# Where the operands of a matmul lie in SBUF, and one plain pair fewer in the second feed-forward stage

## The chip, the cores and the metric

The kernel runs on one core of a Trainium2 chip. The metric is the device time of one execution in microseconds (us), as the median of several runs. A profiled execution gives one trace. The engines are called as in the profile: PE is TensorE's matmul, PEld its weight load, DVE is VectorE, ACT is ScalarE, POOL is GpSimd, SP is the queue that issues most of the DMAs.

## The reference

One encoder layer in float32: 512 positions, width 1024. Two gated feed-forward stages of inner width 2752 stand around a mixer (a Fourier mixer and grouped attention with 8 query and 2 key heads).

```python
x = x + 0.5 * swiglu(rms_norm(x, ffn1_norm), ffn1_w_gate, ffn1_w_up, ffn1_w_down)
h = rms_norm(x, mix_norm)
u = h @ w_in
...                                   # Fourier mixer f_out, attention a_out
x = x + jnp.concatenate([f_out, a_out], axis=-1) @ w_out
x = x + 0.5 * swiglu(rms_norm(x, ffn2_norm), ffn2_w_gate, ffn2_w_up, ffn2_w_down)
return rms_norm(x, final_norm)
# swiglu(h, g, u, d) = (silu(h @ g) * (h @ u)) @ d
```

## The kernel before

All activations lie transposed: x is eight tiles of 128 channels by 512 positions. To keep float32 accuracy at the speed of the float32r format, every operand is split in a high part (rounded) and a low part (the rest), and every product is three matmuls: high by high, high by low, low by high (`product`, L144; the same three by hand at L370). ACT rounds the high parts, and DVE subtracts for the low parts (`lows`, L107). A low part can also be made by a DMA that adds onto the negated high part (`rest_by_dma`, L126), which is issued on POOL's queue.

**Places.** `ring` (L83) holds twelve slots of 1024 float32r words per partition. In a feed-forward stage the first eight hold h (`hh`, `hl`: the high and the low part of a norm's input times its gain) at the start, and the others hold converted weights; later all of them hold weights. `gx` (L92) holds x. Each feed-forward stage opens a pool with `at` (L248: the gated activations, seven places of a high and a low part of 512 columns) and `rt` (L249: seven combinations of h's quarters, high and low, 256 columns each). The mixer opens a pool with `more` (two further weight slots), the tables `chan`, `pos`, and its operands `ks`, `vst`, `e`, `qa`, `qb`; a second pool has `ph` and `pl`, the attention's probabilities. Pools lie one behind another in the order in which they are opened, tiles in the order of their allocation.

**A feed-forward stage** (`ffn`, L240) goes through 21 chunks j of 128 inner columns, a gate and an up chunk each (a pair), and a tail of 64 columns ("t"). They come in the four groups of `GROUPS` (L27).
- The first group's pairs are plain (`gate`, L259): 8 x 3 products of 512 columns for the gate chunk and as many for the up chunk. Some of the weights of this part lie in four places of at that are lent (L467). `n_plain`, the number of members of the first group, counts the plain pairs: chunks 0 to n_plain - 1. Beside them the combinations in rt are made (`operands`, L284), four calls spread over the gates.
- The other pairs go by `seven` (L359): gate and up chunk over the two halves of the positions are made from seven products of 4 x 3 matmuls of 256 columns, with rt moving and combinations of the weights (`prepare`, L318) loaded. A group's `seven` runs one chunk ahead of the group.
- After each group come the down products (`down`, L435) of the group's chunks: eight blocks d, each 3 matmuls of 512 columns for a chunk (2 for the tail), with at moving. Their weights are converted by `weights` (L131) when block d begins. In the last group of the second stage the last three blocks run in two halves of 256 columns (`closing`, L1256).

The order on PE and on SP's queue is the order in which the code is written (`in_order`, L100); ACT, DVE and POOL are ordered by a planner with a model of the times. In the mixer all engines follow the written list `ORDER`.

Of the kernel before, what the change touches and what calls it, by code (L numbers as in the profile page):

```python
# [6 lines left out]
F32 = mybir.dt.float32  # L7
# [6 lines left out]
P = 128  # L14
S = 512
D = 1024
KD = D // P
# [6 lines left out]
WARM = 9  # L24
NS = 12

GROUPS = ((0, "t", 1, 2), range(3, 9), range(9, 15), range(15, 21))  # L27
PLACES = 7
HALF = S // 2
USES = "a11", "a12", "s1", "s2", "s4", "s3", "a22"  # L30
# [48 lines left out]
def encoder(ctx, tc, A, out):  # L79
    nc = tc.nc  # L80
    cp = ctx.enter_context(tc.tile_pool(name="const", bufs=1))
    wp = ctx.enter_context(tc.tile_pool(name="weights", bufs=3))
    ring = cp.tile([P, NS, KD * P], F32R, name="ring")  # L83
    taken = []
    tp = ctx.enter_context(tc.tile_pool(name="temps", bufs=2))
    pp = ctx.enter_context(tc.tile_pool(name="psum", bufs=8, space=bass.MemoryType.PSUM))

# [149 lines left out]
            nc.scalar.copy(self.rb[:, t], pss[1][:, t])  # L237
            return pss[0]

    def ffn(norm, after, wgu, wd, wdt, opening, closing):  # L240

        n_ = norm.n
        n_plain = len(GROUPS[0])
        with tc.tile_pool(name=f"act{n_}", bufs=1) as ap, tc.tile_pool(name=f"sums{n_}", bufs=2) as sp:
            at = ap.tile([P, PLACES, 2, S], F32R, name=f"at{n_}")  # L248
            rt = ap.tile([P, 7, 2, KH, HALF], F32R, name=f"rt{n_}")  # L249
            wt = []  # L250
            free, where = list(range(PLACES)), {}
# [7 lines left out]
            def gate(c, between={}, by_dma=False):  # L259
                whi, wlo = weights(wgu[c], f"gu{n_}_{c}", by_dma=by_dma)  # L260
                ps = bank(f"gu{n_}_{c}")
                for k in range(KD):
                    between.get(k, int)()
                    product(ps, whi[:, k, :], wlo[:, k, :], hh[k], hl[k], k == 0, k == KD - 1)
                return ps
# [18 lines left out]
            def operands(rp, i0, i1):  # L284
                for i in range(i0, i1):
                    b = sp.tile([P, 4, HALF], F32, tag="raw_g", name=f"b{n_}_{i}")
                    for o, k in ((0, i), (2, i + KH)):
                        nc.vector.scalar_tensor_tensor(
                            out=b[:, o : o + 2].rearrange("p a b -> p (a b)"), in0=x[k],
                            scalar=gains[:, norm.n, k : k + 1], in1=rp, op0=ALU.mult, op1=ALU.mult,  # L290
                        )
                    b12, b11, b22, b21 = (b[:, o] for o in range(4))
                    t = sp.tile([P, 4, HALF], F32, tag=("s12", "s34")[i % 2], bufs=1, name=f"t{n_}_{i}")
                    for o, (p, q) in enumerate(((b12, b11), (b22, t[:, 0]), (b22, b12), (b21, t[:, 1]))):
                        nc.vector.tensor_tensor(out=t[:, o], in0=p, in1=q, op=ALU.subtract)
                    for src, c in ((b[:, 1:], slice(0, 3)), (t, slice(3, 7))):
                        h, l = rt[:, c, 0, i], rt[:, c, 1, i]
                        nc.scalar.copy(h, src)
                        if src is t or i < 2 or n_:
                            lows(l, src, h)  # L300
                        else:
                            rest_by_dma(l, h, src)
# [132 lines left out]
            def down(d, group, gi):  # L435

                js = [j for j in group if j != "t"]
                whi, wlo = weights(wd[d][:, js[0] : js[-1] + 1, :], f"dn{n_}_{d}_{gi}", len(js))
                w = wt[d // 4][:, d % 4 * P : (d % 4 + 1) * P]

                def steps(ps, t):
                    for i, j in enumerate(group):
                        h, l = (at[:, where[j], o, t] for o in range(2))
                        first, last = i == 0, i == len(group) - 1
                        if j == "t":
                            nc.tensor.matmul(ps[:, t], w, h, start=first, stop=False)
                            nc.tensor.matmul(ps[:, t], w, l, start=False, stop=last)
                        else:
                            k = j - js[0]
                            product(ps[:, t], whi[:, k, :], wlo[:, k, :], h, l, first, last)  # L450
                        yield

                return steps
# [4 lines left out]
                )  # L458

            every = slice(0, S)  # L460
            for gi, group in enumerate(GROUPS):
                last = gi == len(GROUPS) - 1
                ahead = []
                if gi:
                    rest = seven(range(group[0] + 1, min(group[-1] + 2, NF)), ready)
                else:
                    lent = [at[:, i].rearrange("p a b -> p (a b)") for i in range(PLACES - 4, PLACES)]  # L467
                    plain.extend(lent)
                    row = []
                    pss = dict(enumerate(opening(gate, lambda: norm.column([norm.acc]), lambda: row.append(norm.row()))))  # L470
                    back(lent[:2])
                    due, parts, left = [*pss, "t"], list(range(KH)), range(2 * len(pss), 2 * n_plain)
                    pss["t"] = [gate(2 * NF)]
                    tail_weights()
                    for i, c in enumerate(left):
                        pss.setdefault(c // 2, []).append(gate(c, by_dma=not n_ and i > 0))
                        if due:
                            j = due.pop(0)
                            evacuate(at[:, place(j)], n_, pss[j], norm)
                        if c % 2 and c != left[-1]:  # L480
                            due.append(c // 2)
                        while len(parts) * len(left) > (len(left) - 1 - i) * KH:
                            o = parts.pop(0)
                            operands(row[0], o, o + 1)

                    def rest():
                        evacuate(at[:, place(n_plain - 1)], n_, pss[n_plain - 1], norm)

                def added(d, ps):
                    residual(d, ps, every)  # L490
                    if last:
                        (after.sums if closing else after.add)(d)
                    if ahead:
                        f, *a = ahead.pop(0)
                        f(*a)

                waiting = []
                for d in range(KD):
                    if last and closing and d == KD - 3:
                        closing([(e, down(e, group, gi)) for e in range(d, KD)], residual)  # L500
                        break
                    if last and d == KD - 2:
                        back(lent)
                    ps = bank(f"dn{n_}_{d}_{gi}")
                    steps = down(d, group, gi)(ps, every)
                    for _ in range(len(group) - (last and d < 2)):
                        next(steps)
                    waiting.append((d, ps, steps))
                    if d == 1 and not last:
                        ready = prepare(GROUPS[gi + 1][0] + 1)  # L510
                        ahead.extend(ready[1])
                    if d == 0:
                        rest()
                        if last:

                            lent = slots[KD - 2 : KD]
                            plain[2:2] = lent
                            continue
                    for d_, ps, steps in waiting:
                        for _ in steps:  # L520
                            pass
                        added(d_, ps)
                    waiting = []
                for f, *a in ahead:
                    f(*a)
                if not gi:
                    back(lent)
                free.extend(where[j] for j in group)
# [36 lines left out]
    n0, n1 = Norm(0), Norm(1)  # L565
# [84 lines left out]
        return [pss[0:2], pss[2:4]]  # L650

    with in_order():
        ffn(n0, n1, A["wgu1"], A["wd1"], A["wdt1"], opening1, None)


    n2 = Norm(2)
    with tc.tile_pool(name="mix", bufs=1) as mp, tc.tile_pool(name="mixt", bufs=1) as mt:

        more = mp.tile([P, 2, KD * P], F32R, name="more")
        more = [more[:, i, :] for i in range(2)]  # L660
        plain.extend(more)
# [7 lines left out]
        pos = mp.tile([P, 2, 2, 514], F32R, name="pos")  # L669
        odd = mp.tile([1, 258], F32R, name="odd")  # L670
        sc = mp.tile([P, 4, 10], F32, name="sc")


        ops = {}
# [552 lines left out]
    n3 = Norm(3)  # L1227
# [74 lines left out]
        finish(2, 4, n3.rows, ((0,), (1,), (4, 5), (2, 3), (6, 7)))  # L1302

    with in_order():
        ffn(n2, n3, A["wgu2"], A["wd2"], A["wdt2"], lambda gate, column, row: [[gate(0, {KD - 1: column}), gate(1, {3: row})]], closing)


def _order():
# [106 lines left out]
```

## Time and profile before

| | |
|---|---|
| median of 3 runs | 868.52 us (868.05 to 868.54) |
| the profiled execution, its own time | 868.42 us |
| its span (first to last instruction) | 866.4 us |
| mean granted TensorE clock | 0.997 |
| busy, share of the span | PE 99%, PEld 89%, DVE 74%, ACT 53%, POOL 3% |

Groups of instructions are shown as line, engine, operation, output <- inputs, shapes and count, then the busy time in us and the mean duration of one in ns, then the idle time before them and what ended it. Matmuls are pipelined: the duration of one reaches past the start of the next, so the pace of a stretch is its length divided by the number of products in it. A timeline row gives the start and the length in us. A row by stretch gives the length and then for each engine its busy time and count, the granted clock, the DMA engines' mean busy share and the GB/s they moved.

### The profile page before, as it was taken

Reading aid. Unit: us, or ns where it says so; the run is one execution under the profiler, and the core shown is the slowest. Engines: PE = TensorE matmul, PEld = TensorE weight load, DVE = VectorE, ACT = ScalarE, POOL = GpSimd, SP = SyncE. Lnnn points to the kernel's source line nnn. Section 1 sums busy time; section 2 is a strip of 40 time slices with the busy share of each in tenths; the row PEclk is TensorE's granted clock in tenths of the full one; section 3 lists DMA queues with packets and bytes.
Section 4 is the critical chain, followed back from the end, with each engine's and each line's share of the span. In section 5 each row is a group of like instructions: output and inputs, shape, how many; then the busy total and the mean of one; then the engine's idle time right before and its main releaser. Section 6 shows DMA issues by size and latency. Waiting matters only on the chain.

```text
span 866.4 us, 13588 instructions
## 1 busy us (share of the span) xinstructions
PE 858.6 (99%) x5389; PEld 768.2 (89%) x5389; DVE 641.2 (74%) x1003; ACT 462.9 (53%) x771; POOL 29.8 (3%) x32
## 2 busy tenths in 40 slices
PE   9999999999999999999999999999999999999996
PEld 6878998899989998889988888889998999889986
DVE  6998985488746837699998478978974688459544
ACT  7763763267424635677776346535652366326543
POOL 0110000000000000222000000000000000000001
PEclk9999999999999999999999999999999999999998
DMA  7664322323233113414010223232323232323212
GB/s 244 164 155 155 116 95 65 116 99 132 73 135 114 44 52 110 146 49 135 32 66 25 98 87 108 85 134 98 110 79 128 92 118 84 98 106 101 74 38 98
DMA packets 30480, 87.94 MB, mean 102 GB/s; under 512 B 3664, under 2 KB 8528, under 8 KB 30288
## 3 DMA queue, kind: packets, MB, share of 16 engines
q1 hardware_dynamic: 28320, 82.87, 28.5%
q0 software_dynamic: 1552, 3.68, 2.1%
q8 instruction: 42, 0.69, 0.3%
q10 hardware_dynamic: 544, 0.52, 0.2%
q14 instruction: 22, 0.18, 0.1%
HBM read 83.39 MB, written 2.10 MB: 99 GB/s over the span
## 4 chain that ended last, share of the span: by engine, by line
PE 97%; DVE 1%; DMA 1%; issue 0%; ACT 0%; POOL 0%; POOLq 0%; SPq 0%; DVEq 0%; ACTq 0%
PE r L370 23%; PE q L370 11%; PE dn L147 8%; PE dn L145 8%; PE dn L146 8%; PE p L370 6%; PE mix L145 3%; PE mix L147 3%; PE mix L146 3%; PE gu L145 3%; PE gu L147 3%; PE gu L146 3%; PE gu L618 3%; PE mix L1106 2%; PE mix L1063 2%; PE mix L913 1%
## 5 line engine op out<-in xcount | busy, mean ns | idle before, releaser
L370 PE MATMUL r<-rt,ring 128*128 128x256 f32 x1632 | 213.2, 283 | 0.0
L370 PEld LDWEIGHTS r<-rt,ring 128*128 128x128 f32 x1632 | 201.8, 188 | 2.4
L147 PE MATMUL dn<-at,ring 128*128 128x512 f32 x303 | 119.7, 395 | 0.2 <-DVE ring L108 0.2
L145 PE MATMUL dn<-at,ring 128*128 128x512 f32 x303 | 119.7, 395 | 0.0
L146 PE MATMUL dn<-at,ring 128*128 128x512 f32 x303 | 119.6, 395 | 0.0
L370 PE MATMUL q<-rt,ring 128*128 128x256 f32 x816 | 107.9, 281 | 0.0
L456 DVE SCALAR_TENSOR_TENSOR gx<-dn,gx 128x512 f32<-128x512 f32 x61 | 42.1, 689 | 82.1 <-PE dn L147 82.0
L370 PEld LDWEIGHTS q<-rt,ring 128*128 128x128 f32 x816 | 101.6, 188 | 0.0
L108 DVE TENSOR_TENSOR ring<-s,ring 128x1024 fp32r<-128x1024 f32 x68 | 82.9, 1221 | 17.6 <-PE r L370 10.6
L137 ACT CAST ring<-raw_dn 128x768 fp32r<-128x768 f32 (+1 forms) x59 | 45.5, 775 | 93.3 <-PE dn L146 77.4
L331 ACT CAST ring<-s 128x1024 fp32r<-128x1024 f32 x68 | 71.4, 1051 | 38.2 <-PE r L370 18.3
L147 PEld LDWEIGHTS dn<-at,ring 128*128 128x128 f32 x303 | 57.0, 188 | 14.3 <-DVE ring L108 0.9
L146 PEld LDWEIGHTS dn<-at,ring 128*128 128x128 f32 x303 | 57.0, 188 | 13.0
L145 PEld LDWEIGHTS dn<-at,ring 128*128 128x128 f32 x303 | 57.0, 188 | 13.0
L108 DVE TENSOR_TENSOR ring<-raw_dn,ring 128x768 fp32r<-128x768 f32 (+1 forms) x59 | 51.8, 880 | 7.2 <-ACT ring L137 6.2
L370 PE MATMUL p<-rt,ring 128*128 128x256 f32 x408 | 53.9, 281 | 0.0
L108 DVE TENSOR_TENSOR ring<-raw_g,ring 128x1024 fp32r<-128x1024 f32 x34 | 41.6, 1223 | 16.6 <-PE p L370 11.2
L370 PEld LDWEIGHTS p<-rt,ring 128*128 128x128 f32 x408 | 50.8, 188 | 0.0
L331 ACT CAST ring<-raw_g 128x1024 fp32r<-128x1024 f32 x34 | 35.7, 1049 | 23.1 <-DMA raw_g<-in_wgu 10.0
L340 ACT CAST ring<-raw_u 128x512 fp32r<-128x512 f32 x34 | 21.1, 620 | 38.2 <-PE dn L147 18.8
L415 DVE TENSOR_TENSOR u<-g,u 128x512 f32<-128x512 f32 x34 | 23.4, 687 | 16.0 <-ACT u L414 16.0
L145 PE MATMUL gu<-ring 128*128 128x512 f32 x80 | 31.3, 391 | 0.0
(309 smaller groups left out, 1576.1 us busy)
## 6 DMA issues: line engine op xcount, KB each, us to landing
raw_dn<-in_wd SPq DMA_DIRECT2D x48, 384.0 KB, 3.1
raw_g<-in_wgu SPq DMA_DIRECT2D x34, 512.0 KB, 3.7
raw_u<-in_wgu SPq DMA_DIRECT2D x34, 512.0 KB, 4.4
raw_gu<-in_wgu SPq DMA_DIRECT2D x14, 512.0 KB, 3.5
raw_o<-in_wo SPq DMA_DIRECT2D x8, 512.0 KB, 3.4
raw_dn<-in_wd SPq DMA_DIRECT2D x16, 192.0 KB, 2.4
raw_wq<-in_wins SPq DMA_DIRECT2D x4, 512.0 KB, 4.5
raw_f<-in_winf SPq DMA_DIRECT2D x4, 512.0 KB, 3.5
```

The source lines that it names most:

```text
L108: nc.vector.tensor_tensor(out=lo, in0=src, in1=asf(hi), op=ALU.subtract)
L137: nc.scalar.copy(hi[:, :n, :], raw[:, :n, :])
L145: nc.tensor.matmul(ps, whi, mhi, start=first, stop=False)
L146: nc.tensor.matmul(ps, whi, mlo, start=False, stop=False)
L147: nc.tensor.matmul(ps, wlo, mhi, start=False, stop=last)
L331: nc.scalar.copy(hi, src)
L340: nc.scalar.copy(hi, src)
L370: nc.tensor.matmul(ps, a[:, ks], b[:, i], start=first and i == 0 and o == 0, stop=i == KH - 1 and o == 2, skip_group_check=not first,)
L415: nc.vector.tensor_tensor(out=u, in0=b["g"], in1=u, op=ALU.mult)
L456: nc.vector.scalar_tensor_tensor(out=x[d][:, t], in0=ps[:, t], scalar=0.5, in1=x[d][:, t], op0=ALU.mult, op1=ALU.add)
L618: nc.tensor.matmul(pss[c], w[:, k % 2, c], m[k], start=k == 0 and m is hh and w is hi, stop=k == KD - 1 and w is lo,)
L1063: nc.tensor.transpose(pts[n][:, c * P : (c + 1) * P], prob[t, b, c][:, kc * P : (kc + 1) * P], ident)
```

## The change

A helper `room` allocates n bytes of a partition that nothing uses, which moves all that is allocated behind it. Rooms of 192 bytes stand behind the ring, ahead of at in each feed-forward stage and ahead of `more` in the mixer; one of 64 bytes stands between at and rt, and one of 32 behind `sc` in the mixer.

The second stage gets groups of its own: its first group is (0, "t", 1), so chunks 0 to 2 are plain instead of 0 to 3, and 18 instead of 17 pairs go by `seven`; its last group has seven chunks. In the second stage's opening the low part of one gate's weights (the second of those in the loop) and the low parts of the first three combinations in the last two calls of `operands` are now made by DMA, the latter as in the first stage. In the second stage's first group the weights of the down blocks are converted up to two blocks earlier.

```diff
-GROUPS = ((0, "t", 1, 2), range(3, 9), range(9, 15), range(15, 21))
+GROUPS1 = ((0, "t", 1, 2), range(3, 9), range(9, 15), range(15, 21))
+GROUPS2 = ((0, "t", 1), range(2, 8), range(8, 14), range(14, 21))
...
     taken = []
+
+    def room(pool, n):
+        pool.tile([P, n // 4], F32, name=f"room{len(rooms)}")
+        rooms.append(n)
+
+    rooms = []
+    room(cp, 192)
...
         with tc.tile_pool(name=f"act{n_}", bufs=1) as ap, tc.tile_pool(name=f"sums{n_}", bufs=2) as sp:
+            room(ap, 192)
             at = ap.tile([P, PLACES, 2, S], F32R, name=f"at{n_}")
+            room(ap, 64)
             rt = ap.tile([P, 7, 2, KH, HALF], F32R, name=f"rt{n_}")
...
-                        if src is t or i < 2 or n_:
+                        if src is t or i < 2:
                             lows(l, src, h)
                         else:
                             rest_by_dma(l, h, src)
...
-                        pss.setdefault(c // 2, []).append(gate(c, by_dma=not n_ and i > 0))
+                        pss.setdefault(c // 2, []).append(gate(c, by_dma=i in (1,) if n_ else i > 0))
...
-                waiting = []
+                waiting, downs = [], []
                 for d in range(KD):
...
-                    steps = down(d, group, gi)(ps, every)
+                    while len(downs) < min(d + 1 + (0 if gi or not n_ else 2), KD):
+                        downs.append(down(len(downs), group, gi))
+                    steps = downs[d](ps, every)
...
+        room(mp, 192)
         more = mp.tile([P, 2, KD * P], F32R, name="more")
...
         sc = mp.tile([P, 4, 10], F32, name="sc")
+        room(mp, 32)
```

`ffn` takes its groups as an argument: GROUPS1 in the first stage, GROUPS2 in the second.

More of the change, by code (lines that the diff above doesn't have):

```diff
@@ L238, in rows, with ffn @@
             return pss[0]
-    def ffn(norm, after, wgu, wd, wdt, opening, closing):
+    def ffn(norm, after, wgu, wd, wdt, groups, opening, closing):
         n_ = norm.n
-        n_plain = len(GROUPS[0])
+        n_plain = len(groups[0])
         with tc.tile_pool(name=f"act{n_}", bufs=1) as ap, tc.tile_pool(name=f"sums{n_}", bufs=2) as sp:
+            room(ap, 192)
             at = ap.tile([P, PLACES, 2, S], F32R, name=f"at{n_}")
+            room(ap, 64)
             rt = ap.tile([P, 7, 2, KH, HALF], F32R, name=f"rt{n_}")
@@ L460, in ffn @@
             every = slice(0, S)
-            for gi, group in enumerate(GROUPS):
-                last = gi == len(GROUPS) - 1
+            for gi, group in enumerate(groups):
+                last = gi == len(groups) - 1
                 ahead = []
@@ L509, in ffn @@
                     if d == 1 and not last:
-                        ready = prepare(GROUPS[gi + 1][0] + 1)
+                        ready = prepare(groups[gi + 1][0] + 1)
                         ahead.extend(ready[1])
@@ L652, in encoder @@
     with in_order():
-        ffn(n0, n1, A["wgu1"], A["wd1"], A["wdt1"], opening1, None)
+        ffn(n0, n1, A["wgu1"], A["wd1"], A["wdt1"], GROUPS1, opening1, None)
     n2 = Norm(2)
     with tc.tile_pool(name="mix", bufs=1) as mp, tc.tile_pool(name="mixt", bufs=1) as mt:
+        room(mp, 192)
         more = mp.tile([P, 2, KD * P], F32R, name="more")
@@ L1304, in encoder @@
     with in_order():
-        ffn(n2, n3, A["wgu2"], A["wd2"], A["wdt2"], lambda gate, column, row: [[gate(0, {KD - 1: column}), gate(1, {3: row})]], closing)
+        ffn(n2, n3, A["wgu2"], A["wd2"], A["wdt2"], GROUPS2, lambda gate, column, row: [[gate(0, {KD - 1: column}), gate(1, {3: row})]], closing)
 def _order():
```

## The prediction, made before the change was run

> **What bounds the kernel now.** I read the page first: the engines, the chain that ended last, and the groups.
>
> ```profile
> span 866.4 us, 13588 instructions
> PE 858.6 (99%) x5389; PEld 768.2 (89%) x5389; DVE 641.2 (74%) x1003; ACT 462.9 (53%) x771; POOL 29.8 (3%) x32
> ...
> PEclk9999999999999999999999999999999999999998
> ...
> PE 97%; DVE 1%; DMA 1%; issue 0%; ACT 0%; POOL 0%; POOLq 0%; SPq 0%; DVEq 0%; ACTq 0%
> ```
>
> PE holds 97% of the chain at an almost full clock. So the time is, to a few us, a sum over PE's products of the time from one start to the next. Removing a wait elsewhere can gain almost nothing; changing the pace of a product changes everything. The durations in the groups include the drain that overlaps the next product, so I use them only to compare kinds and take the pace from starts and counts. The counts:
>
> ```profile
> L370 PE MATMUL r<-rt,ring 128*128 128x256 f32 x1632 | 213.2, 283 | 0.0
> ...
> L147 PE MATMUL dn<-at,ring 128*128 128x512 f32 x303 | 119.7, 395 | 0.2 <-DVE ring L108 0.2
> ...
> L370 PE MATMUL q<-rt,ring 128*128 128x256 f32 x816 | 107.9, 281 | 0.0
> ...
> L370 PE MATMUL p<-rt,ring 128*128 128x256 f32 x408 | 53.9, 281 | 0.0
> ...
> L145 PE MATMUL gu<-ring 128*128 128x512 f32 x80 | 31.3, 391 | 0.0
> ```
>
> The 256-column products against rt number 1632 + 816 + 408 = 2856. The 512-column products of the down stage (dn) number 3 x 303 = 909 in the shown form (L145 and L146 have the same count). The grouping that keeps forms apart adds the rest:
>
> ```profile
> L145 PE MATMUL dn<-at 128*128 128x512 f32 x15 | 5.9, 395 | 0.0
> ...
> L446 PE MATMUL dn<-at,wt 128*128 128x512 f32 x16 | 6.3, 394 | 0.0
> ...
> L145 PE MATMUL gu<-ring,at 128*128 128x512 f32 x32 | 12.7, 396 | 0.0
> ...
> L618 PE MATMUL gu<-ring,at 128*128 128x512 f32 x48 | 11.8, 398 | 0.0
> ```
>
> With 3 x 15 whose weights lie in lent places of at and 2 x 16 against the tail weights, dn has 986. The gates have 3 x 32 and 48 products with weights in at.
>
> Now the pace. The timeline of PE in the second stage's opening shows whole gates, each 8 x 3 = 24 products, one after another without a pause; these are the first rows of four of them:
>
> ```profile
> 525.84 0.40 PE L145 MATMUL gu<-ring,at 128*128 128x512 f32 x1
> ...
> 531.43 0.39 PE L145 MATMUL gu<-ring 128*128 128x512 f32 x1
> ...
> 536.88 0.39 PE L145 MATMUL gu<-ring 128*128 128x512 f32 x1
> ...
> 542.33 0.40 PE L145 MATMUL gu<-ring,at 128*128 128x512 f32 x1
> ```
>
> The same operation on the same moving operand takes 5.59 us for 24 products (232.9 ns each) when the weights lie in a slot lent from at, and 5.45 us (227.1 ns) when they lie in the ring. Only the place differs. From the kernel's allocations, in bytes of a partition modulo 256: ring and with it h begin at 128; at, rt and more at 0; the tail weights at 192; the mixer's operands (ks, vst, e, qa, qb, ph, pl) at 224. Ring against ring is a distance of 0, ring against at is 128. The down stage has at (0) moving against ring weights (128) all through. The busy time by stretch, for two stretches of whole down blocks (six blocks of 18 products, 108; the counts take in the products that overlap an edge) and one of 256-column products:
>
> ```profile
> core 0: us, PE busy (x) PEld busy (x) DVE busy (x) ACT busy (x) POOL busy (x), PEclk, DMA share, GB/s
> 145.67:170.87 25.20, 25.20 (x109) 20.27 (x108) 11.08 (x15) 5.80 (x7) 0.00 (x0) 1.00 0.35 115
> 653.40:678.60 25.20, 25.20 (x110) 20.27 (x109) 11.68 (x16) 5.81 (x7) 0.00 (x0) 1.00 0.34 115
> 584.80:643.60 58.80, 58.80 (x493) 58.56 (x492) 50.02 (x72) 35.56 (x61) 0.00 (x0) 1.00 0.29 99
> ```
>
> 25.20 / 108 = 233.3 ns at distance 128, as in the gates that read at. And 58.80 / 492 = 119.5 ns for the 256-column products, also at distance 128.
>
> **The change part by part: places of the 512-column products.** The rooms move everything behind the ring by 192 bytes, and the pools of at and more by 192 again, so at and more come to 128, the tail weights to 128, and the mixer's operands (with 32 more) to 128: distance 0 for all. What I expect is the pace of the ring-ring gate, 227.1 ns.
> - Down stage: 986 x (233.3 - 227.1) = 6.1 us.
> - Gates with weights in at: 144 x 5.8 = 0.8 us.
> - The mixer's output products, 8 x 8 x 3 = 192 at distances 96 and 224. Their group stands at 395 ns beside 391 for gu from the ring, the same step as dn's:
>
> ```profile
> L145 PE MATMUL mix<-qa,ring 128*128 128x512 f32 x20 | 7.9, 395 | 0.0
> ```
>
> So 192 x 6 = 1.2 us. The scores and the attended products (128 by the code) have both operands at 224 already; 0.
> Sum: -8.1 us, all of it on PE, where nothing hides it. Bounds: 0 if the gates' difference had another cause, -8.9 if those 128 gain 6 ns too, by the change of their neighbours.
>
> A rule speaks against this whole part. The Trainium skill, "SBUF — State Buffer", section "Who interferes with whom", gives TensorE two independent read ports and says that "PE and ACT never wait on anyone"; by it places are worth 0. The trace differs: 232.9 against 227.1 ns for the same gate with its weights in two places.
>
> **Places of the 256-column products.** rt comes to 192, a distance of 64 from the ring's weights, where it is 128 now. No long run at 64 stands in the trace. The nearest are the Fourier products with pos moving (at offsets 8, 24, 8, 16, 32, 16) and e at 224 as weights: distances 40, 56, 40, 48, 64, 48. One of their runs in PE's timeline:
>
> ```profile
> 457.05 0.28 PE L145 MATMUL mix<-pos,eh 128*128 128x256 f32 x1
> 457.17 0.28 PE L146 MATMUL mix<-pos,eh 128*128 128x256 f32 x1
> 457.29 0.28 PE L147 MATMUL mix<-pos,el 128*128 128x256 f32 x1
> 457.40 0.28 PE L145 MATMUL mix<-pos,eh 128*128 128x256 f32 x1
> 457.52 0.28 PE L146 MATMUL mix<-pos,eh 128*128 128x256 f32 x1
> 457.63 0.28 PE L147 MATMUL mix<-pos,el 128*128 128x256 f32 x1
> ```
>
> From start to start: 0.12, 0.12, 0.11, 0.12 and, at 64, 0.11 us; the five together take 0.58 us, 116 ns each. The pace at 64 lies between 110 to 115 ns (the one row, to its rounding) and today's 119.5 from below; from above, a bad place could cost as much as it does the 512-column products, 5.8 ns more, so 125. I take 115: next to the run's 116, pulled to the row at 64 itself. 2856 x (119.5 - 115) = 12.9 us gained. Ends: 18.6 us gained at 113, 16.6 us lost at 125.3.
>
> **The second stage with three plain pairs.** One pair of gates, 48 products of 512 columns, goes (48 x 227.1 = 10.9 us), and seven products of 4 x 3 with 256 columns come (84 x 115 = 9.7 us): -1.2 us. The down products stay the same in number; the last group has 7 members for 6, so three blocks done in halves take 9 x (2 x 119.5 - 227.1) = 0.1 us more. The three down weights prepared ahead add no instruction; they move conversions of ACT and DVE earlier. I cost this at 0 because PE is not waiting for them now.
>
> What can show is DVE. Its busy time by stretch, for the gates after the opening pair and for the first down group:
>
> ```profile
> 525.84:564.40 38.56, 38.56 (x169) 31.60 (x168) 37.19 (x59) 21.13 (x29) 0.00 (x0) 1.00 0.26 88
> 564.40:584.80 20.40, 20.40 (x89) 16.55 (x88) 15.77 (x25) 6.66 (x10) 0.00 (x0) 1.00 0.42 143
> ```
>
> DVE works 37.19 of 38.56 us here, the one place where it is close to PE. The change takes from it, by the groups of this stage in the order of the code, the lows of three gates (two gone, one by DMA), one evacuation of four, and the lows of two operand blocks:
>
> ```profile
> L108 DVE TENSOR_TENSOR ring<-raw_gu,ring 128x1024 fp32r<-128x1024 f32 x5 | 6.1, 1219 | 1.2 <-ACT ring L137 1.2
> ...
> L108 DVE TENSOR_TENSOR rt<-b,rt 128x768 fp32r<-128x768 f32 x4 | 3.8, 953 | 0.0
> ...
> L538 DVE TENSOR_TENSOR u2p<-g2p,u2p 128x512 f32<-128x512 f32 x4 | 2.7, 687 | 0.0
> ```
>
> 3 x 1.22 + 4 x 0.69 + 2 x 0.95 = 8.3 us, which leaves 28.9. PE's five gates take 5 x 5.45 = 27.3 us. The down group after them has 8 x 8 products, 14.5 us, against a DVE load of 15.8 less about 1 for the smaller weights. So DVE falls behind by 1.6 us, and by about 2 at the end of the group, where rt must be ready. The seven-product stretch behind it has 50.0 us of DVE in 492 x 115 = 56.6 us and catches up. I put 1.5 us on PE, between 0 (the weights are prepared that far ahead) and 5. The DMAs that take over the lows go to POOL's queue, where POOL's busy time is 0.00 in both stretches, so nothing is queued behind them; ACT gets the two negated copies per block in their stead and has 17 us free in the first stretch.
>
> **The sum.** 868.4 (the profiled execution; its span is 866.4, and it is 0.1 under the median of 868.52) - 8.1 - 12.9 - 1.2 + 0.1 + 1.5 = 847.8 us.
>
> **The rivals.**
> 1. The 256-column products don't care about 64 or 128: 119.5 stays. For it: 256-column products with both operands in the ring, at distance 0, have about the duration of those against rt (282 beside 281 to 283), so this width could be bound by something else. Against: the 0.11 us at 64. 868.4 - 8.1 - 0.9 + 0.1 + 0.5 (DVE has more time) = 860.0 us.
>
> ```profile
> L914 PE MATMUL mix<-ring 128*128 128x256 f32 x48 | 13.6, 282 | 0.0
> ```
>
> 2. DVE becomes the bound in the second stage. Against rt at 115 the seven-product stretch runs DVE at 88%, with a backlog of 2 us at its start; if ring slots then come free too late, PE waits at each of six pairs for about 1 us. 847.8 + 6 = 853.8 us.
> 3. Places do nothing, or the rooms don't land where the allocations say: only the pair counts, -0.9 and up to 1.5 of DVE. About 868.5 us, no change that can be measured (0.2%, 1.7 us, is about what a measurement of this kernel can tell from none). The gates speak against it. The Trainium skill's rule of two independent ports, told above, would give this rival.
> 4. Slower: 64 is a bad distance for 256 columns. Price: the step between good and bad places, 5.8 ns, on 2856 products = 16.6 us, less 8.1, and the pair at 84 x 125.3 = 10.5 against 10.9: 868.4 - 8.1 + 16.6 - 0.4 + 0.1 = 876.6 us. It decides from 122.5 ns up, where 2940 products at 3 ns more eat the 8.1 us and the pair's 0.8. For it: another of the short Fourier runs shows 0.12 us at 64, between these two rows. Against: no row at 40 to 64 reaches 125.
>
> ```profile
> 456.34 0.28 PE L146 MATMUL mix<-pos,eh 128*128 128x256 f32 x1
> 456.46 0.28 PE L147 MATMUL mix<-pos,el 128*128 128x256 f32 x1
> ```
>
>
> **How the numbers follow.** Forecast 0.53, rival 1 0.20, rival 2 0.14, rival 3 0.05, rival 4 0.08. Faster by over 0.2% is the forecast with rivals 1 and 2: 0.87; within 0.2% rival 3: 0.05; slower rival 4: 0.08. The range reaches below to 113 ns with no wait (868.4 - 8.1 - 18.6 - 1.4 = 840.3, and 0.8 more if the mixer's 128 follow: 839) and above to rival 1 with 1 us more: 861.
>
> **What would show it.** Down blocks: 18 products in 4.09 us instead of 4.20, and the dn groups' duration at gu's 391. Gates that read at: as long as those that read only the ring. The seven-product stretches: 492 products in some 56.6 us; 55.6 would be 113 ns, 58.8 rival 1, over 60 rival 4. DVE: over 95% busy from the gates to the first seven-product group of the second stage, and idle time of PE there of some 1.5 us in front of weights or rt; 5 or more is rival 2. Mixer: shorter by 1 to 2 us. The forecast is wrong if down blocks keep 4.20 us, or if 256-column products pace over 118.

## The result and the profile after

The changed kernel takes 856.59 us (median of 4 runs, 855.34 to 857.20) against 868.53 us: ratio 0.9862, 95% interval 0.9844 to 0.9879. That is 11.9 us less, where 20.7 were forecast. The profiled execution took 856.85 us. Its page, the parts that answer to those of before:

```profile
span 855.1 us, 13706 instructions
PE 846.4 (99%) x5434; PEld 765.5 (90%) x5434; DVE 641.5 (75%) x1007; ACT 467.9 (55%) x781; POOL 33.3 (4%) x35
...
PE 97%; DVE 1%; DMA 0%; issue 0%; ACT 0%; POOL 0%; POOLq 0%; DVEq 0%; ACTq 0%
...
L382 PE MATMUL r<-rt,ring 128*128 128x256 f32 x1680 | 216.8, 280 | 0.0
...
L157 PE MATMUL dn<-at,ring 128*128 128x512 f32 x300 | 117.0, 390 | 0.5 <-DVE ring L118 0.5
...
L382 PE MATMUL q<-rt,ring 128*128 128x256 f32 x840 | 109.8, 279 | 0.0
```

PE still is the chain, with 45 products more and 12 us less of busy time. The down products' duration fell from 395 to 390 ns, where the gates from the ring had been. PE's timeline in the second stage's opening, first rows of four gates (24 products each), two reading weights in at and two in the ring:

```profile
520.23 0.39 PE L155 MATMUL gu<-ring,at 128*128 128x512 f32 x1
...
525.67 0.39 PE L155 MATMUL gu<-ring 128*128 128x512 f32 x1
...
531.11 0.39 PE L155 MATMUL gu<-ring 128*128 128x512 f32 x1
...
536.55 0.39 PE L155 MATMUL gu<-ring,at 128*128 128x512 f32 x1
```

All are 5.44 us apart now; before, those from at took 5.59. The busy time by stretch: two stretches of 108 down products; two seven-product stretches of 492 products, the first of the first stage and the first of the second; then the second stage's five gates and its first down group:

```profile
core 0: us, PE busy (x) PEld busy (x) DVE busy (x) ACT busy (x) POOL busy (x), PEclk, DMA share, GB/s
144.42:168.94 24.52, 24.52 (x110) 20.29 (x109) 11.12 (x15) 5.87 (x7) 0.00 (x0) 1.00 0.34 119
628.61:653.12 24.51, 24.51 (x110) 20.28 (x109) 11.72 (x16) 5.87 (x7) 0.00 (x0) 1.00 0.34 118
76.40:134.80 58.40, 58.40 (x494) 58.11 (x492) 50.66 (x73) 36.12 (x62) 0.00 (x0) 1.00 0.29 100
561.98:619.00 57.02, 57.02 (x494) 56.62 (x493) 52.38 (x77) 35.19 (x61) 0.00 (x0) 1.00 0.31 107
520.20:547.40 27.20, 27.20 (x121) 22.53 (x120) 26.45 (x46) 18.36 (x27) 3.50 (x3) 1.00 0.53 120
547.40:562.00 14.60, 14.60 (x66) 11.94 (x64) 14.55 (x25) 7.58 (x12) 0.00 (x0) 1.00 0.52 172
```

Down products go at 24.52 / 108 = 227.0 ns. DVE is full in the last two rows, 26.45 of 27.20 and 14.55 of 14.60 us, and PE is busy all through. The seven-product stretches take 58.40 and 57.02 us, 118.7 and 115.9 ns a product with their stops. Here is the second of them, in the chain in order of time (start, length; 12 products in a row):

```profile
566.40 1.41 PE r L382 x12
567.81 1.41 PE q L382 x12
569.23 3.02 PE r L382 x24
572.25 1.41 PE p L382 x12
...
577.90 1.41 PE q L382 x12
579.31 2.91 PE r L382 x24
582.23 1.36 PE p L382 x12
583.59 1.36 PE r L382 x12
584.95 1.36 PE q L382 x12
```

There are two paces at the same distance of 64. The stretch begins at 1.41 us for 12 (117.8 ns from start to start) and goes on at 1.36 (113.3 ns, every step 113 or 114) to its end. The change comes at 579.31, in a row of 24 products that is longer than twice 1.41 or 1.36: PE stops there for some 0.2 us. The other five stretches of this execution stay at 1.41. From here on a pace of 117.8 or 113.3 is a mean without stops.

### The profile page after: what moved, and what is told of

It reads as the page before. It is cut to its first block, busy times and chain, and to the rows that moved or that the text cites. A ratio compares the mean times of both kernels' runs of the same rounds, so it can differ in the third digit from the quotient of the medians.

```text
span 855.1 us, 13706 instructions
## 1 busy us (share of the span) xinstructions
PE 846.4 (99%) x5434; PEld 765.5 (90%) x5434; DVE 641.5 (75%) x1007; ACT 467.9 (55%) x781; POOL 33.3 (4%) x35
## 4 chain that ended last, share of the span: by engine, by line
PE 97%; DVE 1%; DMA 0%; issue 0%; ACT 0%; POOL 0%; POOLq 0%; DVEq 0%; ACTq 0%
PE r L382 23%; PE q L382 12%; PE dn L157 8%; PE dn L155 8%; PE dn L156 8%; PE p L382 6%; PE mix L155 3%; PE mix L157 3%; PE mix L156 3%; PE gu L632 3%; PE gu L155 2%; PE gu L157 2%; PE gu L156 2%; PE mix L1122 2%; PE mix L1079 2%; PE mix L928 1%
## 5 line engine op out<-in xcount | busy, mean ns | idle before, releaser
L382 PE MATMUL r<-rt,ring 128*128 128x256 f32 x1680 | 216.8, 280 | 0.0
L382 PEld LDWEIGHTS r<-rt,ring 128*128 128x128 f32 x1680 | 205.6, 188 | 2.6
L157 PE MATMUL dn<-at,ring 128*128 128x512 f32 x300 | 117.0, 390 | 0.5 <-DVE ring L118 0.5
L155 PE MATMUL dn<-at,ring 128*128 128x512 f32 x300 | 117.0, 390 | 0.0
L156 PE MATMUL dn<-at,ring 128*128 128x512 f32 x300 | 116.7, 389 | 0.0
L382 PEld LDWEIGHTS q<-rt,ring 128*128 128x128 f32 x840 | 103.5, 188 | 0.0
L118 DVE TENSOR_TENSOR ring<-s,ring 128x1024 fp32r<-128x1024 f32 x70 | 85.3, 1220 | 16.5 <-PE r L382 10.5
L147 ACT CAST ring<-raw_dn 128x768 fp32r<-128x768 f32 (+3 forms) x58 | 45.5, 787 | 87.0 <-PE dn L156 70.6
L343 ACT CAST ring<-s 128x1024 fp32r<-128x1024 f32 x70 | 73.5, 1050 | 34.8 <-PE r L382 17.9
L157 PEld LDWEIGHTS dn<-at,ring 128*128 128x128 f32 x300 | 56.3, 188 | 13.0 <-DVE ring L118 1.1
L156 PEld LDWEIGHTS dn<-at,ring 128*128 128x128 f32 x300 | 56.3, 188 | 11.3
L155 PEld LDWEIGHTS dn<-at,ring 128*128 128x128 f32 x300 | 56.3, 188 | 11.3
L118 DVE TENSOR_TENSOR ring<-raw_dn,ring 128x768 fp32r<-128x768 f32 (+3 forms) x58 | 51.6, 892 | 6.1 <-ACT ring L147 4.1
L224 POOL TENSOR_TENSOR r<-ms,mhalf 128x4 f32<-128x4 f32 (+1 forms) x5 | 5.9, 1179 | 679.9 <-DVE ms L217 679.9
```

What stands on the lines that cost most here:

```text
L118: nc.vector.tensor_tensor(out=lo, in0=src, in1=asf(hi), op=ALU.subtract)
L147: nc.scalar.copy(hi[:, :n, :], raw[:, :n, :])
L155: nc.tensor.matmul(ps, whi, mhi, start=first, stop=False)
L156: nc.tensor.matmul(ps, whi, mlo, start=False, stop=False)
L157: nc.tensor.matmul(ps, wlo, mhi, start=False, stop=last)
L343: nc.scalar.copy(hi, src)
```

## The experiments

**The change in four parts.** Two theories: the pace follows the places (the gain is in the rooms), or the planner's new order and the shorter opening bring it (the gain is in the groups).

groups_only: `room` allocates nothing, the rest is the change.

```diff
-        pool.tile([P, n // 4], F32, name=f"room{len(rooms)}")
         rooms.append(n)
```

> The second stage's groups and DMAs of the change without any room: every operand lies as before. If the gain comes from the places (theory), this is 868.5 less 48 gates' products at 229 ns plus 84 at 119.5: about 867.5 us, within 1 us, with down blocks of 18 products at 4.20 us. If the gain comes from the shorter opening and the work moved off DVE (rival), it is 862 us or less.

Measured 867.70 us against 868.65, ratio 0.9990 (0.9981 to 1.0000). The groups alone give about 1 us (0 to 1.6), as expected.

rooms_only: all rooms, with the groups and DMAs of before.

```diff
-GROUPS2 = ((0, "t", 1), range(2, 8), range(8, 14), range(14, 21))
+GROUPS2 = GROUPS1
...
-                        if src is t or i < 2:
+                        if src is t or i < 2 or n_:
...
-by_dma=i in (1,) if n_ else i > 0
+by_dma=not n_ and i > 0
...
-(0 if gi or not n_ else 2)
+0
```

> All rooms, with the groups and the DMAs of before. Theory: 512-column products at 227 ns (7 us) and 256-column products at 117.8 ns, as in most of the changed kernel's stretches (0.9 to 1.3 ns on 2856, 3 to 4 us): 857 to 859 us. If one seven-product stretch falls into the pace of 113.3 that one stretch of the changed kernel shows, up to 2 us less. Rival (groups): 866 us or more.

Measured 858.38 us, ratio 0.9884 (0.9870 to 0.9899). The gain is in the places. As in the changed kernel, one of the six stretches changes to 113.3 on its way, though it is the fifth here and the fourth there.

rooms_rt128: rooms_only with rt at its old distance.

```diff
-            room(ap, 64)
+            room(ap, 128)
```

> All rooms, but 128 bytes between at and rt in place of 64, so that rt is 128 off the ring as before; groups of before. Theory: the 512-column part alone, 868.5 - 7 = 861.5 us, and no stretch of 256-column products at 113.3 ns. If the distance of 64 does nothing beyond chance, it equals rooms_only within 0.5 us.

Measured 862.42 us, ratio 0.9928 (0.9912 to 0.9945): the 512-column part alone is worth 6.2 us. No stretch goes at 113.3; twelve products take 1.44 us:

```profile
76.34 0.23 PE dn L157
76.56 1.44 PE r L382 x12
78.00 1.44 PE p L382 x12
```

So rt at 64 was worth 4.0 us of rooms_only. What lies behind rt moves by 64 bytes as well, but PE doesn't read it. That the place of rt alone moves the time doesn't fit the rule of two independent read ports (the Trainium skill, "SBUF — State Buffer", "Who interferes with whom").

rt64_only: the kernel before with one room between at and rt.

```diff
             at = ap.tile([P, PLACES, 2, S], F32R, name=f"at{n_}")
+            ap.tile([P, 48], F32, name=f"room{n_}")
             rt = ap.tile([P, 7, 2, KH, HALF], F32R, name=f"rt{n_}")
```

> One room of 192 bytes between at and rt and nothing else: rt at 64 off the ring, all else where it was. Theory: 2856 products at 117.8 instead of 118.7 between their pauses, 865 to 866 us, and 256-column stretches that are at 117.8 or 113.3 and at nothing else; down blocks stay at 4.20 us. If the pace of 113.3 is met often from the old down pace, as low as 856. If 64 is worth nothing alone: 868.5.

Measured 862.98 us (861.96 to 865.95), ratio 0.9940 (0.9920 to 0.9959): 5.7 us, where 2.5 to 3.5 were expected for 117.8 ns alone. That is more than the 4.0 in the presence of the other rooms, but the runs spread over 4 us, where the kernel before spreads over 1.5. In its trace 59 of 238 rows of twelve products (rows that hold no stop) go at 113.3 ns, in the changed kernel 26 of 245. All six stretches start at 117.8, though the down products ahead of them keep their old pace (232.4 ns on average; seven in 1.62 us here):

```profile
169.00 0.23 PE dn L147
...
170.39 0.23 PE dn L147
170.62 1.41 PE r L371 x12
172.03 1.41 PE p L371 x12
```

**The distances.** Three kernels, each run once, with at and rt elsewhere in each stage, by the numbers in the two rooms ahead of at and rt (the diff shows the first of the three).

```diff
-            room(ap, 192)
+            room(ap, 224 if n_ == 0 else 256)
...
-            room(ap, 64)
+            room(ap, 224 if n_ == 0 else 224)
```

> The changed kernel with other places in the feed-forward stages. First stage: at 32 off the ring, rt at 0; second: at 64 off, rt at 32. Theory (pace by place modulo 256): 0 is the best place for 512 columns, so down products at 232 to 234 ns in both stages; 256-column products at 0 settle at 120.0 as the Fourier projections do, and at 32 between 113 and 120. Rival (only 0 and 128 differ, or the places of the tiles don't matter beyond the ring): the same pace in both stages.

> As the scan before, with at and rt both 96 off the ring in the first stage and both 160 off in the second. Theory: down products at 233.3 ns at 96, as the mixer's output products showed at that distance, and 231 to 234 at 160; 256-column products between 117 and 121, unless one of the two distances holds the pace of 113.3 ns throughout, which would make the second or the first stage's seven-product stretches 4% shorter.

> As the scans before, with at and rt both 192 off the ring in the first stage and both 224 off in the second. Theory: down products at 230 to 234 ns at 192 and at 233.3 at 224, as the mixer's products showed; 256-column products between 117 and 121. If the paces were only a matter of 32-byte steps within a line and not of the distance modulo 256, 192 would equal 0 (227 and 120 ns).

They took 863.96, 867.77 and 860.64 us. The down products fell outside what was expected at one distance: 229.0 ns at 64, not 232 to 234. The finding is the first stage of the third, also against the expectation: its seven-product stretches start at 113.3 ns and mostly stay there, 164.9 us for 1428 products against 169.6 in the changed kernel. Chain in order of time, the last down products and the start of a stretch:

```profile
76.31 0.23 PE dn L157
76.54 0.24 PE dn L155
77.00 0.23 PE dn L157
77.24 1.37 PE r L382 x12
78.60 1.36 PE p L382 x12
79.96 1.37 PE q L382 x12
```

Three runs followed from it.

```diff
 # rt192
-            room(ap, 64)
+            room(ap, 192)
 # all_shifted
+    cp.tile([P, 16], F32, name="roomfirst")
     ring = cp.tile([P, NS, KD * P], F32R, name="ring")
 # fine_16: at 16 and 240, rt 176 and 208 off the ring, by other rooms and a first element 4 words (16 bytes) into longer tiles
```

> The changed kernel with rt 192 off the ring in both stages (192 bytes between at and rt in place of 64), at still at 0. Theory (192 lets the seven-product stretches settle at 113.3 ns more often than 64): 1428 x 115.5 in the first stage (164.9 us against 169.6) and 1512 x 115.5 in the second (174.6 against 178.0): 856.6 - 8 = 848.5 us, within 3 us as the stretches fall. Down blocks stay at 227 ns. Rival (the first stage of the scan was 113.3 by chance, or because at stood 192 off too): 854 to 857 us with most stretches at 117.8.

Measured 851.43 us (849.25 to 852.27), ratio 0.9797 (0.9780 to 0.9814). Faster than the changed kernel by 5.2 us, at the edge of what was expected: against the expectation all six stretches start at 117.8. All six change to 113.3 later; one of them falls back to 117.8 for good, one for a time.

> The changed kernel with 64 bytes more ahead of the ring: every place moves by 64, every distance stays. Theory (the distance between the moving operand and the weights sets the pace): gates and down blocks at 227 ns and 256-column stretches at 117.8 or 113.3 only, about 857 us. Rival (the address itself, such as h and at at 128 modulo 256, sets it): down blocks at another pace, 230 to 234 ns, 863 us or more.

858.29 us in one run, down products at 227.1 ns and all stretches at 117.8: with every address moved by 64 and every distance kept, the paces stayed. At this one shift it is the distance, not the address, that counts.

> The changed kernel with steps of 16 bytes: at 16 off the ring and rt 176 off in the first stage, at 240 off and rt 208 off in the second. If the pace changes by steps of 64 bytes, 176 behaves like 160 (117 to 118.6 ns) and 208 like 192 (mostly 113.3), and at at 240 like 224 (233) but at 16 like 0 (227). If by 16 bytes, at 16 is slower than 227 as well and 208 falls back from 113.3.

864.64 us in one run. The steps are finer than 64 bytes. At 208 no row of twelve products goes at 113.3 any more. For 512 columns 16 costs 4.5 ns, as one of the two cases had it, but 240 is as good as 0, which neither had.

The paces from start to start in these traces, as the mean without steps that hold a stop (over 250 and 130 ns). The down products are those with weights in the ring. Most columns rest on one stage of one execution:

| distance | 0 | 16 | 32 | 64 | 96 | 128 | 160 | 176 | 192 | 208 | 224 | 240 |
|---|---|---|---|---|---|---|---|---|---|---|---|---|
| 512 columns, down, ns | 227.1 | 231.6 | 233.4 | 229.0 | 233.4 | 232.8 | 234.2 | | 233.2 | | 233.2 | 227.0 |
| 256 columns, seven, ns | 119.9 | | 117.2 | 117.8 or 113.3 | 120.0 | 118.7 | 117.8 | 119.2 | 117.8 or 113.3 | 119.2 | 118.3 | |

The distances are counted modulo 256. By the allocations, counted modulo 512, h lies 0 off the ring's weights and at 256 off in the changed kernel, and products with either moving go at 227 ns; rt lies 64 off in rt64_only and 320 off in the changed kernel, and both show the same two paces.

**What decides between the two paces.** In every trace a stretch with rt at 64 or 192 holds its pace for dozens of products and changes only at a stop of PE. With rt at 192 its first pace goes with the place of at: 117.8 with at at 0 (down products at 227.0 ns ahead), 113.3 with at at 192 (233.2 ahead). With rt at 64 it is 117.8 in every trace, with at at 0 and, in rt64_only, at 128 (232.4 ahead). So the slower pace of the down products doesn't bring 113.3 by itself. Whether that pace counts at all, or rather that at and rt lie at the same distance, no run here separates.

The stops come in the first three pairs of a group, ahead of the sixth of the pair's seven products (of twelve matmuls each). That product writes the bank from which ACT copies u2, and ACT has a cast of the next weights first; ACT's timeline in the changed kernel:

```profile
577.86 1.05 ACT L343 CAST ring<-s 128x1024 fp32r<-128x1024 f32 x1 [0.97 <-PE r L382]
578.82 0.37 ACT L390 COPY u<-r 128x256 f32<-128x256 f32 x1
```

PE's next product starts at 579.24, behind the copy's end. Two kernels give the weights' pieces another spread, so that the copy comes first, one with at at 0 and one with at at 192; rt is at 192 in both:

```diff
-PIECES = (0, 2, 2, 1, 1, 1, 1)
+PIECES = (0, 2, 1, 0, 2, 2, 1)
 # rt192_u2first: room(ap, 192) ahead of at, room(ap, 192) ahead of rt
 # at192_u2first: room(ap, 128) ahead of at, room(ap, 256) ahead of rt
```

> rt192 with the pieces of the next pair's weights spread (0, 2, 1, 0, 2, 2, 1) in place of (0, 2, 2, 1, 1, 1, 1), so that ACT copies u2 before it casts the next s34, and PE doesn't stop ahead of the sixth product of a pair. Theory (the pace of a seven-product stretch is handed on, from the down products at 227 ns it starts at 117.8, and only PE's stops let it change): with the stops gone all stretches stay at 117.8, 2940 x 117.8 = 346.3 us for 342.6 in rt192's profile, and the time rises to some 855 us although 18 stops of 0.2 us are gone. Rival (192 leads to 113.3 by itself, with time): the stops' 3.5 us are gained and the share of 113.3 grows, 848 us or less.

Measured 851.89 us (851.23 to 852.09), ratio 0.9804 (0.9788 to 0.9820); 855 was expected, without stops. One stop of three is left in each group, now in the fourth pair (the third in the shorter group). In all six groups the stretch keeps 117.8 up to this stop, for over 220 products, and goes at 113.3 behind it, so time alone doesn't change the pace:

```profile
202.06 1.41 PE r L382 x12
203.47 1.41 PE q L382 x12
204.89 2.93 PE r L382 x24
207.82 1.36 PE p L382 x12
209.18 1.36 PE r L382 x12
```

> As rt192_u2first, but at too lies 192 off the ring, so that the down products go at 233.2 ns and the seven-product stretches follow on that. Theory: as in the first stage of the scan at 192, every stretch starts at 113.3, and without stops it stays there: 2940 x 113.3 = 333.1 us, 9.5 less than rt192's profile, against some 1000 products of 512 columns at 6.1 ns more (6.1 us) and the gates that read at (0.5 us): about 848.5 us, and 6 us or more below rt192_u2first. Rival (the pace doesn't depend on what ran before): slower than rt192_u2first by 6 us.

Measured 850.22 us (849.91 to 850.78), ratio 0.9787 (0.9772 to 0.9801), the lowest median of these kernels. Its slowest run is faster than the fastest of rt192_u2first. 848.5 was expected. All six stretches start at 113.3 and stay there, past the one stop too:

```profile
168.18 0.24 PE dn L155
168.65 0.24 PE dn L157
168.89 1.36 PE r L382 x12
170.25 1.36 PE p L382 x12
171.61 1.36 PE q L382 x12
...
202.89 1.36 PE q L382 x12
204.25 2.99 PE r L382 x24
207.24 1.36 PE p L382 x12
208.60 1.36 PE r L382 x12
```

Of the 245 rows of twelve, one, which stands alone between down blocks, goes at 117.8. The 2940 products take 334.9 us, for 342.7 in rt192_u2first's trace, and the down products give back 6.1. So the gap to rt192_u2first is 1.7 us and not 6: the stops that were left had already brought that kernel to 113.3 for over a third of its products.

## Why the prediction was right or wrong

**What bounds the kernel: right.** PE held 97% of the chain before and after, and the kernels differ in pace, in the number of products and in a few short stops of PE. groups_only, which changes planner, DMAs and DVE's load but no place, moved 1 us.

**512-column products: right in kind and pace, a quarter too large.** The pace came out at 227.0 ns, as read from the gates. The part alone gave 6.2 us for 8.1 (rooms_rt128). Summed from start to start in the traces of before and rooms_rt128, the down stage gained 4.9 us for the 6.1 of the working (230.0 to 225.1), the gates with weights in at 0.8 and the mixer 1.3, as forecast; 0.3 us were lost again in the 256-column products. The mis-sized factor is 233.3 ns, taken from two stretches: the mean over all down products that don't stop was 232.7, so that a product gained 5.5 ns and not 6.2, which is 0.7 us. The other 0.5 us are stops, which grew; PE's idle time at dn in front of DVE's weights in the first stage went from 0.2 us to 0.5. The working also has at against ring weights, at 128, all through. By the allocations 45 of the 986 down products, with their weights in at, stood at 0 already. They still went from 230.9 ns to 226.7 (rooms_rt128): in runs of three to six between other products, a product's own distance doesn't give its pace.

**256-column products: the step that failed.** Forecast: from 119.5 to 115 ns, 12.9 us. Measured: 4.0 us (rooms_only against rooms_rt128). Two things were wrong. First, today's 119.5 ns holds PE's stops, 18 of them and 2.4 us in all, which the change doesn't remove; without them the pace at 128 was 118.7, so even 115 would have gained 10.6 us. Second, no stretch goes at 115: 64 has two paces, and with at at 0 the stretches enter the slower one, 117.8. I took a mean between a single step and its neighbours at other distances for the pace of a long run. The step at 64 was 113 ns in that run and 122 ns in the one shown for rival 4; that the 113 was a sight of the faster pace isn't shown. Of the 4.0 us, 2.6 are the 0.9 ns from 118.7 to 117.8, and some 1.5 the one stretch that changed to 113.3, which nothing in the working foresaw. The bound that the working named for the good case, 113, is what at192_u2first runs at; the forecast's error was to think that the distance of rt alone decides it.

The prediction named its own sign of being wrong: 256-column products over 118 ns. By its measure, a stretch's length divided by its products, four of the five stretches of 492 took 58.4 us, 118.7 ns, and only the one that changed to 113.3 took 57.0.

**The pair: right.** Gates and products to the account of -1.1 us (forecast -1.2, and 0.1 for the halves); measured 1.0 alone, and 1.8 between rooms_only and the changed kernel, within what is uncertain as long as a stretch can take either of two paces.

**DVE's 1.5 us: not paid.** DVE did fill up as worked out, but the weights are made early enough: from start to start PE lost 0.2 us in the second stage's gates, as before, and 0.05 us in its down products. After the kernel's start, the only idle of PE in front of DVE stands in the first stage.

**Rivals.** 856.6 lies nearer to rival 1 (860.0: the 256-column products don't care) than to the forecast. The products cared, by a third of what was forecast. Rival 2's waits and rival 4's loss don't show; rival 3 falls by rooms_rt128.

## What to carry to other kernels

Where PE is the chain from end to end, take the pace of each kind of product from starts and counts, and compare like products whose operands lie in different places: a difference of 2.6% between two such gates led to a gain that no wait in the profile pointed at. Take both paces of a forecast the same way, with stops or without. A pace read from a few products in a row is a candidate, not a forecast; a long run can settle elsewhere, and a price for it needs a long run at the same distance. When two kernels differ by places, look at the steps from start to start before looking for a cause in the schedule.

## What the runs showed of the hardware

- The pace of back-to-back float32r products with a weight load each depends on the distance modulo 256 between the moving operand and the weights: 227.0 to 234.2 ns for 512 columns, 113.3 to 120.0 for 256. The best distances differ: 0 or 240 for 512; 64 or 192 for 256, where 113.3 was reached. This holds for long runs; 45 products at 0 in short runs between others went at 230.9 ns (the kernel before). The smallest paces stand above the gap of an isolated matmul that the Trainium skill gives ("TensorE: Matmul & The Clock Gate", "Back-to-back issue gap": N / 2.4 + 2.5 ns, an estimate of 215.8 and 109.2 ns); no run here reached it.
- At distances of 64 and 192 there are two steady paces, 117.8 and 113.3 ns. With rt at 192, the place of at decided which one a stretch starts at. Stops of PE of 0.1 to 0.5 us switched it, from 117.8 to 113.3 or back, and other stops of such a length didn't. That this is why equal runs of rt64_only differ by up to 4 us is likely but not shown, as only one of its executions has a trace.
- Why the distance matters, and what a stop shifts, the traces don't show. That it is a conflict between the reads of the two operands is an argument and not tried.
